# A decoder step with a 16384-expert mixer: the gate matrix grouped by 8 in DRAM, the sample's top-k on 128 partitions, PSUM copies of 8 tokens

## The chip, the cores and the metric

One core of a Trainium2 chip. The time is device microseconds of one execution; it is the median of three runs of the kernel. Engines are called TensorE (PE in the rows; PEld is its weight load), VectorE (DVE), ScalarE (ACT), GpSimd (POOL) and SyncE (SP, which here only issues DMAs).

## The reference

One layer for 512 prompt tokens and 64 sample tokens, width 1024: attention over three dilated windows beside a short gated convolution, an output projection, then a mixer of 16384 single-neuron experts, and a final norm. Only the mixer matters here. For each token and each of 8 heads:

```
q = (x @ wq) as 8 heads x 2 halves x 128
s = q . sub_keys                      128 scores per half
sv, si = top_k(s, 16)                 per half
cand = sv0[:, None] + sv1[None, :]    16 x 16 sums, top 16 of them
e = si0 * 128 + si1 of the winners;  g = softmax(top)
out = sum over 8 x 16 winners of  g * gelu(x . u[e]) * v[e]
```

## The kernel before, in words

The tokens are five blocks: 0 to 3 of 128 prompt tokens, and block 4, the 64 sample tokens. Blocks 0 and 4 take the mixer by gathering: for each winner a row of `u` and a row of `v` are fetched by an indirect DMA (`gather_units`, L464), and VectorE multiplies and adds them (tiles `jk` at L477 and `accg` at L487). Blocks 1 to 3 (`DENSE`, 384 tokens) take it densely: all 16384 experts are computed in 128 chunks of 128, and a matrix of gates, almost all zero, weighs them.

The stages around the change, in the order of the program:

1. `group(GB, ...)` (L576): output projection and norm of blocks 1 to 4; then the loop of L690 over 16 parts of `wq`: projection, scores (L703), a copy of the scores out of PSUM (L705, L707), and `topk1` (L490), five VectorE instructions per block and part. Block 4 has 64 tokens, so its instructions run on 64 partitions.
2. The gate build, `gbuild` (L812), for each dense block: `topk2` (L501) finds the 16 winners of each head. Then for each 8 tokens VectorE makes one-hot matrices `oj` and `oi` (L844, L848), ScalarE makes a third (L852, 8 instructions of 128 elements), TensorE multiplies them token by token into `pG` in PSUM (L857, L858, 128x128 each), and ScalarE copies `pG` to the tile `stg` (L860). A `stg` of 32 tokens goes to the DRAM tensor `Gd` (L863), 12 of them in all.
3. Between these stand the u-steps, `ustep` (L773): load a 128-expert chunk of `ut` (tile `ur`), split it on ScalarE (`uh`) and VectorE (`ul`), 24 multiplications into `pu` (L107 to L109), Gelu on ScalarE (tile `a`, L782), and for the first 62 chunks a store to `Ad`. 68 chunks run ahead of the last stage (`LAG`); `unext` calls them from the gate build by a count of debt.
4. `topk_gather` (L559) for block 4: `topk2` on 64 partitions, 8 heads; three DMAs then bring half of the slots to partitions 64 to 127 so that the gather uses all 128.
5. The v-loop (L935): for chunks 68 to 127 a u-step and a v-step, then for chunks 0 to 67 a v-step alone. A v-step (`vprep`, L885) loads `v`, loads the gates of four chunks at a time (`gt`, L891), multiplies them with the activations (tile `w`, L898), splits, and makes 18 multiplications of 512 columns into the accumulators `y` (L909 to L913).

`pump` (L448) places gather steps between all of these by a count of credit. The order of the instructions on each engine is not the order of the code: a scheduler with its own idea of times (L1031) sets it once, when the program is built. Each engine then works through its list in order. DMAs are issued from SyncE's list, those of the gather from GpSimd's.

The lines that matter most:

```
Gd = dram.tile([NTB, P, NCH, TB], F32, name="Gd")                      # L86: 12 x 128 x 128 x 32
pg_ = psG.tile([P, 4, P], F32, name="pG")                              # L854: 4 tokens, one PSUM bank
nc.scalar.activation(stg[:, :, tl:tl + 4].rearrange("p i t -> p t i"), pg_, AF.Copy, scale=1.0 / GSC)   # L860
nc.sync.dma_start(gt, Gd[:, :, i0:i0 + 4, :].rearrange("b j i t -> j b i t"))                           # L891
```

`stg` is [128, 128, 32]: the copy of L860 reads `pG` word after word and writes each word 128 bytes behind the last.

Of the kernel before, what the change touches and what calls it, by code (L numbers as in the profile page):

```python
# [19 lines left out]
P = 128  # L20
# [47 lines left out]
def body(tc, I, O):  # L68
# [12 lines left out]
    biasp = keep.tile([P, 4, P], F32, name="biasp")  # L81
# [4 lines left out]
    Gd = dram.tile([NTB, P, NCH, TB], F32, name="Gd")  # L86
# [28 lines left out]
    abp = pool(ab, "ab", side="right")  # L115
    qT = abp.tile([P, NPAIR, 512], F32, name="qT")
# [297 lines left out]
    zl = small.tile([P, 2, 18], F32, name="zl", bufs=1)  # L414
# [5 lines left out]
    zo = small.tile([P, 256], F32, name="zo", bufs=1)  # L420
# [69 lines left out]
    def topk1(st, cc, b, n, src):  # L490
        hd_, p_ = divmod(cc, 2)
# [9 lines left out]
    def topk2(st, b, n, ef, gat):  # L501
        sv, si = st[b]
        sf = tk.tile([P, 8, 2, 16], F32, name="sf")
        nc.vector.tensor_copy(sf[:n], si[:n])
        nc.vector.tensor_scalar(sf[:n, :, 0, :], sf[:n, :, 0, :], 128.0, None, op0=OP.mult)
        cand = tk.tile([P, 8, NCAND], F32, name="cand")
        cid = tk.tile([P, NCAND, 8], I16, name="cid")
        for src, dst in ((sv, cand), (sf, cid.rearrange("p w h -> p h w"))):
            o = 0
            for (a0, a1_, nb_) in PAIRS:  # L510
                na = a1_ - a0
                out = dst[:n, :, o:o + na * nb_].rearrange("p h (a b) -> p h a b", b=nb_)
                i0 = src[:n, :, 0, a0:a1_].unsqueeze(3).to_broadcast([n, 8, na, nb_])
                i1 = src[:n, :, 1, 0:nb_].unsqueeze(2).to_broadcast([n, 8, na, nb_])
                nc.vector.tensor_tensor(out, i0, i1, op=OP.add)
                o += na * nb_
            yield 1.2
        tv = tk.tile([P, 8, 16], F32, name="tv")
        tp = tk.tile([P, 8, 16], U32, name="tp")
        wc = tk.tile([P, NCAND], F32, name="wc", bufs=2)  # L520
        for hd_ in range(8):
            src = cand[:n, hd_, :]
            nc.vector.max(tv[:n, hd_, 0:8], src)
            nc.vector.match_replace(wc[:n], tv[:n, hd_, 0:8], src, -3.0e38)
            nc.vector.max(tv[:n, hd_, 8:16], wc[:n])
            nc.vector.max_index(tp[:n, hd_, 0:8], tv[:n, hd_, 0:8], src)
            nc.vector.max_index(tp[:n, hd_, 8:16], tv[:n, hd_, 8:16], wc[:n])
# [12 lines left out]
        yield 1.0  # L540
        efv = ef[:n].rearrange("p (h k) -> p h k", h=8)
        for k0 in (0, 8):
            w = FIRST[k0 + 7] + 1
            oh = tk.tile([P, NCAND, 8, 8], I16, name="oh")
            ohf = oh.rearrange("p w k h -> p w (k h)")
            sel = tf[:n, k0:k0 + 8, :].rearrange("p k h -> p (k h)").unsqueeze(1).to_broadcast([n, w, 64])
            nc.vector.tensor_tensor(ohf[:n, :w], iotaw[:n, :w], sel, op=OP.is_equal)
            yield 1.7
            nc.vector.tensor_tensor(oh[:n, :w], oh[:n, :w], cid[:n, :w].unsqueeze(2).to_broadcast([n, w, 8, 8]),
                                    op=OP.mult)  # L550
            yield 1.7
# [483 lines left out]
```

## Time and profile before

| | |
|---|---|
| time, median of 3 runs | 1880.66 us (1880.13 to 1886.15) |
| the profiled execution, span from first to last instruction | 1882.2 us |
| busy: TensorE, VectorE, ScalarE, GpSimd | 1738.2, 1430.9, 881.6, 579.0 us |
| mean granted TensorE clock | 0.955 of full |
| gate build, 816 to 1078 us | TensorE 231.2, VectorE 215.6, ScalarE 253.8 us busy of 262 |
| copies `stg` | 96, 101.2 us |
| DRAM traffic | 485.65 MB read, 45.63 MB written |

The page gives the span and no other time of the profiled execution; it is 1.5 us above the median of the runs. A stretch of the span is read with the view that gives each engine's busy time in it: where one engine is busy nearly all of the stretch, the others wait for it sooner or later; where TensorE is, its work alone sets the length. The view of waits then says who waited for whom. TensorE's busy time counts matmuls that overlap, so a group's mean duration (344 ns for `pu`) is longer than the distance from one to the next.

### The profile page before, as it was taken

What the parts mean: (1) busy time and instruction counts of PE and PEld (TensorE: products, weight loads), DVE (VectorE), ACT (ScalarE), POOL (GpSimd) and SP (SyncE); (2) the same over time, 40 slices, a digit from 0 to 9 for tenths busy, and PEclk for the clock granted to TensorE, in tenths of its full rate; (3) what the DMA queues carried; (4) which work ended last, traced back from release to release, by engine and by line L of the source; (5) the groups of instructions that cost most, each with busy time, mean ns of one, the idle gap of its engine ahead of it and who ended that gap; (6) DMA issues with size and microseconds to landing.
All of it is one profiled execution on the core that took longest, in us unless ns stands there. A gap on an engine that the chain in (4) does not pass through costs nothing. (4 is left out here: it accounts for less than half of the span.)

```text
span 1882.2 us, 29066 instructions
## 1 busy us (share of the span) xinstructions
PE 1738.2 (92%) x10391; PEld 1467.3 (78%) x10391; DVE 1430.9 (76%) x3064; ACT 881.6 (47%) x1615; POOL 579.0 (31%) x483
## 2 busy tenths in 40 slices
PE   7999899997679999988988999999999999999997
PEld 5778655654558998987978889999999997777776
DVE  5433235766888999998788578888888778888888
ACT  4222366645323333479999933333333333333334
POOL 1010201014554214311212234544444444333330
PEclk9999979978788999999999999999999999999999
DMA  4257569858898448867777699999999999999996
GB/s 143 100 181 288 208 245 337 316 185 291 302 320 302 154 143 312 277 216 267 266 261 250 253 365 330 353 335 348 331 336 341 320 361 334 363 344 367 340 349 210
DMA packets 199077, 533.75 MB, mean 284 GB/s; under 512 B 17586, under 2 KB 82660, under 8 KB 197268
## 3 DMA queue, kind: packets, MB, share of 16 engines
q1 hardware_dynamic: 133364, 294.22, 44.0%
q0 software_dynamic: 65568, 237.69, 35.5%
q8 instruction: 81, 1.33, 0.3%
q14 instruction: 64, 0.52, 0.1%
HBM read 485.65 MB, written 45.63 MB: 282 GB/s over the span
## 5 line engine op out<-in xcount | busy, mean ns | idle before, releaser
L469 POOL DMA_INDIRECT row<-in_u,idxg x192 | 257.9, 1343 | 457.6 <-DVE avg L477 231.4
L469 POOL DMA_INDIRECT row<-in_v,idxg x192 | 264.5, 1377 | 421.6 <-DVE accg L487 345.3
L107 PE MATMUL pu<-x2h,uh 128*128 128x384 f32 x1024 | 350.9, 343 | 21.4 <-ACT a L782 11.1
L109 PE MATMUL pu<-x2h,ul 128*128 128x384 f32 x1024 | 352.0, 344 | 7.5 <-DVE ul L104 7.3
L108 PE MATMUL pu<-x2l,uh 128*128 128x384 f32 x1024 | 348.8, 341 | 0.0
L103 ACT ACTIVATE vh<-vr 128x1024 fp32r<-128x1024 f32 x128 | 135.8, 1061 | 290.4 <-PE y L913 251.4
L477 DVE CUSTOM_DVE_ANT_0 jk<-row,x2g 128x1024 bf16<-128x1024 f32 x192 | 233.8, 1218 | 28.0 <-DMA row<-in_u,idxg 26.8
L487 DVE SCALAR_TENSOR_TENSOR accg<-row,avg,accg 128x1024 f32<-128x1024 f32 x190 | 243.2, 1280 | 7.7 <-DMA row<-in_v,idxg 6.7
L909 PE MATMUL y<-vh,wh 128*128 128x512 f32 x768 | 224.7, 395 | 15.5 <-ACT wh L103 15.5
L911 PE MATMUL y<-vl,wh 128*128 128x512 f32 x768 | 234.2, 393 | 0.0
L107 PEld LDWEIGHTS pu<-x2h,uh 128*128 128x128 f32 x1024 | 196.5, 192 | 27.1 <-ACT a L782 12.2
L104 DVE TENSOR_TENSOR vl<-vr,vh 128x1024 fp32r<-128x1024 f32 x128 | 156.6, 1224 | 77.9 <-ACT vh L103 74.9
L913 PE MATMUL y<-vh,wl 128*128 128x512 f32 x768 | 215.6, 390 | 0.0
L109 PEld LDWEIGHTS pu<-x2h,ul 128*128 128x128 f32 x1024 | 196.4, 192 | 12.4 <-DVE ul L104 10.1
L103 ACT ACTIVATE uh<-ur 128x1024 fp32r<-128x1024 f32 x128 | 136.0, 1064 | 145.1 <-PE pu L108 74.1
L108 PEld LDWEIGHTS pu<-x2l,uh 128*128 128x128 f32 x1024 | 196.3, 192 | 1.7
L104 DVE TENSOR_TENSOR ul<-ur,uh 128x1024 fp32r<-128x1024 f32 x128 | 156.2, 1220 | 35.9 <-ACT uh L103 34.2
L909 PEld LDWEIGHTS y<-vh,wh 128*128 128x128 f32 x768 | 143.9, 189 | 46.5 <-ACT wh L103 19.5
L911 PEld LDWEIGHTS y<-vl,wh 128*128 128x128 f32 x768 | 145.1, 189 | 30.4
L913 PEld LDWEIGHTS y<-vh,wl 128*128 128x128 f32 x768 | 144.0, 188 | 30.1
L104 DVE TENSOR_TENSOR wlo<-wraw,whi 128x1024 fp32r<-128x1024 f32 (+1 forms) x96 | 91.0, 952 | 67.5 <-ACT whi L103 67.1
L103 ACT ACTIVATE whi<-wraw 128x1024 fp32r<-128x1024 f32 (+1 forms) x96 | 79.8, 840 | 124.3 <-PE mm L109 53.7
(281 smaller groups left out, 2936.4 us busy)
## 6 DMA issues: line engine op xcount, KB each, us to landing
ur<-in_ut SPq DMA_DIRECT2D x128, 512.0 KB
vr<-in_v SPq DMA_DIRECT2D x128, 512.0 KB
kt<-in_ck SPq DMA_DIRECT2D x60, 512.0 KB
vt<-in_cv POOLq DMA_DIRECT2D x60, 512.0 KB
Gd<-stg SPq DMA_DIRECT2D x12, 2048.0 KB
gt<-Gd SPq DMA_DIRECT2D x32, 768.0 KB
wraw<-in_w_in SPq DMA_DIRECT2D x24, 512.0 KB
Ad<-a SPq DMA_DIRECT2D x62, 192.0 KB
```

Of the source, the lines that this page charges most:

```text
L103: nc.scalar.activation(hi, src, AF.Copy)
L104: nc.vector.tensor_tensor(lo, src, hi.bitcast(F32), op=OP.subtract)
L107: nc.tensor.matmul(out, ah, bh, start=first, stop=False)
L108: nc.tensor.matmul(out, ah, bl, start=False, stop=False)
L109: nc.tensor.matmul(out, al, bh, start=False, stop=last)
L469: nc.gpsimd.indirect_dma_start(out=r, out_offset=None, in_=I[src], in_offset=bass.IndirectOffsetOnAxis(ap=idx[:, s:s + 1], axis=0))
L477: nc.vector.tensor_tensor_reduce(jk, r, x2, 1.0, 0.0, OP.mult, OP.add, av[:, s:s + 1]))
L487: nc.vector.scalar_tensor_tensor(acc, r, av[:, s:s + 1], acc, op0=OP.mult, op1=OP.add))
L909: nc.tensor.matmul(accs[b][k], wh[:, sl], vh[:, k * 512:k * 512 + 512], start=first, stop=False)
L911: nc.tensor.matmul(accs[b][k], wh[:, sl], vl[:, k * 512:k * 512 + 512], start=False, stop=False)
L913: nc.tensor.matmul(accs[b][k], wl[:, sl], vh[:, k * 512:k * 512 + 512], start=False, stop=last)
```

## The change

Five edits:

- `Gd` gets the layout [16 groups of 8 chunks, 128, 12, 8, 32]. A store of `stg` becomes 16 pieces of 1 KB per partition where it was one of 16 KB; a load of gates (`gate_load`) brings a whole group of 8 chunks, 12 KB in a row per partition, where it was 12 pieces of 512 bytes for 4 chunks. There are 17 loads (the group of chunk 68 is read in two halves) where there were 32, and each is asked for four chunks ahead of its first use.
- Block 4's first top-k pass handles heads 0 to 3 on partitions 0 to 63 and heads 4 to 7 on partitions 64 to 127: the parts of `wq` come in the order 0, 8, 1, 9, ..., scores of the second of a pair are written to the upper partitions, and one `topk1` does both. `topk2` runs for it with 4 heads on 128 partitions, and two of the three DMAs that spread the slots go.
- `pG` holds 8 tokens (two PSUM banks), and one ScalarE copy does all 8: it writes 8 words in a row and reads words 512 bytes apart.
- The `ones` operand of the sums of squares in `group` has one column instead of 128.
- `biasp`, `zl` and `zo` come from other pools.

```diff
+GG = 8
-    ones = keep.tile([P, P], F32, name="ones")
+    ones = keep.tile([P, 1], F32, name="ones")
-    Gd = dram.tile([NTB, P, NCH, TB], F32, name="Gd")
+    Gd = dram.tile([NCH // GG, P, NTB, GG, TB], F32, name="Gd")
...
     def topk1(st, cc, b, n, src):
-        hd_, p_ = divmod(cc, 2)
+        hd_, p_ = divmod(cc % 8 if b == 4 else cc, 2)
...
-    def topk_gather(st, b, n, k):
...
+    def topk_gather(st, b, H, k):
+        ef = tk.tile([P, SLOTS], F32, name="ef", bufs=2)[:, :16 * H]
+        if H < 8:
+            nc.sync.dma_start(x2g[k][64:128, :], x2g[k][:64, :])
+        yield from topk2(st, b, H, ef, gatg[k][:, :16 * H])
+        nc.vector.tensor_copy(idxg[k][:, :16 * H], ef)
...
-                    nc.tensor.matmul(ss[:n, bi * P:bi * P + P], sq[:, c - c0, t0 - g0:t0 - g0 + n], ones,
+                    nc.tensor.matmul(ss[:n, bi:bi + 1], sq[:, c - c0, t0 - g0:t0 - g0 + n], ones,
...
-        for cc in range(16):
+        for cc in [c for lo in range(8) for c in (lo, lo + 8)]:
...
+                r0 = up_ if n < P else 0
+                nc.tensor.matmul(p2[r0:r0 + n, bi, :], qc[:, t0 - g0:t0 - g0 + n], skT[:, cc, :], start=True, stop=True)
+            nc.scalar.activation(sc, p2[:, :nb - 1, :], AF.Copy)
+            if not up_:
+                sc4 = gp.tile([P, P], F32, name="sc4", bufs=2)
+            nc.scalar.activation(sc4[up_:up_ + 64, :], p2[up_:up_ + 64, nb - 1, :], AF.Copy)
+            for bi, b in enumerate(grp[:-1]):
+                topk1(st, cc, b, P, sc[:, bi, :])
+            if up_:
+                topk1(st, cc, 4, P, sc4)
...
-                    nc.scalar.activation(stg[:, :, tl:tl + 4].rearrange("p i t -> p t i"), pg_, AF.Copy,
-                                         scale=1.0 / GSC)
+                nc.scalar.activation(stg[:, :, q * TQ:q * TQ + TQ], pg_.rearrange("p t i -> p i t"), AF.Copy,
+                                     scale=1.0 / GSC)
...
-            nc.sync.dma_start(Gd[di * (P // TB) + tb], stg)
+            nc.sync.dma_start(Gd[:, :, di * (P // TB) + tb].rearrange("g j i t -> j g (i t)"),
+                              stg.rearrange("p (g i) t -> p g (i t)", i=GG))
...
+    def gate_load(n_):
+        if n_ >= NCH or order[n_] in gtile or (n_ and order[n_ - 1] // GG == order[n_] // GG):
+            return
...
+        gt = vp.tile([P, NTB, GG, TB], F32, name="gt")
+        nc.sync.dma_start(gt[:, :, k0:k1], Gd[i0 // GG][:, :, k0:k1])
...
         vh, vl = load_split(I["v"][i * P:(i + 1) * P, :], vp, "v")
...
+        gate_load(n_)
+        gate_load(n_ + GG // 2)
+        gt = gtile.pop(i)
```

The scheduler is run anew, so the lists of all engines change. Three places of them follow.

ScalarE, the first tokens of the gate build before (`oi` are the third one-hot matrices of 8 tokens, `uh` and `a` belong to a u-step, `stg` is the copy):

```order
L852 ACTIVATE oi_7168<-oi_7166,gl 128x32x4 x8
L103 ACTIVATE uh<-ur 128x1024
L782 ACTIVATE a<-pu 128x384
L860 ACTIVATE stg<-pG 128x4x128 x2
L852 ACTIVATE oi_7241<-oi_7239,gl 128x32x4 x8
```

And now:

```order
L847 ACTIVATE oi_7126<-oi_7124,gl 128x32x4 x8
L103 ACTIVATE uh<-ur 128x1024
L777 ACTIVATE a<-pu 128x384
L852 ACTIVATE stg<-pG 128x128x8
L847 ACTIVATE oi_7197<-oi_7195,gl 128x32x4 x8
L852 ACTIVATE stg<-pG 128x128x8
L847 ACTIVATE oi_7230<-oi_7228,gl 128x32x4 x8
```

Two copies of 4 tokens became one of 8, and some groups of 8 tokens have no u-step between them.

ScalarE, the end of the gate build before (`vh` and `wh` open the v-loop):

```order
L860 ACTIVATE stg<-pG 128x4x128 x2
L103 ACTIVATE uh<-ur 128x1024
L782 ACTIVATE a<-pu 128x384
L103 ACTIVATE uh<-ur 128x1024
L782 ACTIVATE a<-pu 128x384
L103 ACTIVATE uh<-ur 128x1024
L103 ACTIVATE vh<-vr 128x1024
L103 ACTIVATE wh<-w 128x384
```

And now, the first rows of 33 that stand between the last copy and the first `wh`:

```order
L852 ACTIVATE stg<-pG 128x128x8
L103 ACTIVATE uh<-ur 128x1024
L777 ACTIVATE a<-pu 128x384 x3
L103 ACTIVATE uh<-ur 128x1024 x2
L103 ACTIVATE vh<-vr 128x1024
L777 ACTIVATE a<-pu 128x384 x2
L103 ACTIVATE vh<-vr 128x1024
L103 ACTIVATE uh<-ur 128x1024 x2
```

Behind the gate build there were 3 splits `uh` before the v-loop, and there are 15. Counted over TensorE's whole list, its 3072 multiplications into `pu` stand so (before, now): up to the last score multiplication of L703 83 and 25; from there to the first `pG` 663 and 529; from the first to the last `pG` 912 and 757; from there to the first `y` 94 and 385; in the v-loop 1320 and 1376. VectorE's list, likewise: gather steps ahead of the first `topk1` of blocks 1 to 4, 57 and 67; from there to the first `oj`, 44 and 28; from the first to the last `oj`, 34 and 27. Splits `ul` in the last two stretches: 27 and 20, then 39 and 31.

SyncE, in the v-loop, before:

```order
L891 DMA gt<-Gd 128x12x128
L767 DMA vr<-in_v 128x1024 x2
L896 DMA ar<-Ad 128x384 x2
```

And now:

```order
L887 DMA gt<-Gd 128x3072
L762 DMA vr<-in_v 128x1024 x2
L898 DMA ar<-Ad 128x384 x2
```

The load of gates keeps its place ahead of the loads of `v` and of the stored activations `ar`, in half as many places and with twice the bytes.

## Rows read from the trace of the kernel before

**Rows 1.** The page's first part: span, and each engine's busy time.

```profile
span 1882.2 us, 29066 instructions
PE 1738.2 (92%) x10391; PEld 1467.3 (78%) x10391; DVE 1430.9 (76%) x3064; ACT 881.6 (47%) x1615; POOL 579.0 (31%) x483
```

**Rows 2.** Busy time by stretch: length, PE, PEld, DVE, ACT, POOL (instructions), clock, DMA, GB/s.

```profile
440.00:586.00 146.00, 107.47 (x557) 78.47 (x558) 117.38 (x230) 52.63 (x100) 74.58 (x60) 0.80 0.90 322
586.00:816.00 230.00, 219.76 (x1195) 207.43 (x1196) 223.02 (x893) 83.22 (x139) 71.18 (x50) 0.99 0.67 223
816.00:1078.00 262.00, 231.15 (x1691) 218.84 (x1691) 215.58 (x441) 253.84 (x552) 55.80 (x32) 0.94 0.72 255
1078.00:1093.00 15.00, 15.00 (x89) 15.00 (x88) 4.85 (x4) 6.01 (x8) 0.00 (x0) 1.00 0.93 339
1093.00:1571.00 478.00, 474.83 (x2386) 429.60 (x2384) 395.12 (x450) 169.94 (x230) 223.95 (x169) 1.00 0.95 340
1571.00:1868.00 297.00, 284.72 (x1231) 232.74 (x1232) 248.90 (x317) 108.01 (x144) 100.47 (x77) 0.99 0.96 342
```

**Rows 3.** One stretch, `pu` alone (PE, PEld, ACT), then `pG` alone (PE, ACT).

```profile
816.00:1078.00 262.00, 183.83 (x917) 166.26 (x918) 19.36 (x39) 0.94 0.72 255
...
816.00:1078.00 262.00, 62.34 (x768) 100.21 (x96) 0.94 0.72 255
```

**Rows 4.** Waits of PE, 800 to 1110 us: total, times, longest.

```profile
PE pG L857 <- ACT stg L860: 11.8, 15, 5.1
PE pu L107 <- ACT a L782: 11.1, 5, 2.8
```

**Rows 5.** Timeline of ACT, 880 to 886 us: start, duration, instruction.

```profile
882.35 1.08 ACT L103 ACTIVATE uh<-ur 128x1024 fp32r<-128x1024 f32 x1
...
883.66 2.10 ACT L860 ACTIVATE stg<-pG 128x512 f32<-128x512 f32 x2
885.52 2.46 ACT L852 ACTIVATE oi<-oi,gl 128x128 f16<-128x128 f16 x8
```

**Rows 6.** Timeline of PE, first and last of ten multiplications into `pG`.

```profile
919.83 0.22 PE L857 MATMUL pG<-oi,oj 128*128 128x128 f16 x1
...
920.39 0.23 PE L858 MATMUL pG<-oi,oj 128*128 128x128 f16 x1
```

**Rows 7.** ACT groups by shape: count, busy us, mean ns, idle before them.

```profile
L103 ACT ACTIVATE vh<-vr 128x1024 fp32r<-128x1024 f32 x128 | 135.8, 1061 | 290.4 <-PE y L913 251.4 <-issue 28.2 <-DMA vr<-in_v 7.3
...
L860 ACT ACTIVATE stg<-pG 128x512 f32<-128x512 f32 x96 | 101.2, 1163 | 5.0 <-PE pG L858 5.0
...
L264 ACT ACTIVATE PTs<-sT 128x512 f32<-128x512 f32 x24 | 14.2, 591 | 11.2 <-PE sT L259 11.1
...
L332 ACT ACTIVATE kT<-pT 128x256 f32<-128x256 f32 x5 | 1.9, 390 | 5.0 <-PE pT L320 5.0
...
L328 ACT ACTIVATE qbd<-pT 64x256 f32<-64x256 f32 x2 | 0.8, 378 | 1.7 <-PE pT L320 1.7
```

**Rows 8.** DVE groups by shape: count, busy us, mean ns.

```profile
L477 DVE CUSTOM_DVE_ANT_0 jk<-row,x2g 128x1024 bf16<-128x1024 f32 x192 | 233.8, 1218 | 28.0 <-DMA row<-in_u,idxg 26.8 <-DVE sv L497 0.3 <-DVE rdp L203 0.2
...
L104 DVE TENSOR_TENSOR ul<-ur,uh 128x1024 fp32r<-128x1024 f32 x128 | 156.2, 1220 | 35.9 <-ACT uh L103 34.2 <-PE pu L109 1.4
...
L515 DVE TENSOR_TENSOR cid<-sf 128x64 int16<-128x64 f32 x8 | 5.3, 663 | 0.0
...
L495 DVE MAX8 sv<-scs 64x8 f32<-64x128 f32 x16 | 4.4, 275 | 0.0
...
L515 DVE TENSOR_TENSOR cand<-sv 128x64 f32<-128x64 f32 x8 | 1.7, 212 | 0.0
...
L531 DVE CAST tf<-tp 128x128 int16<-128x128 uint32 x4 | 1.2, 292 | 0.0
...
L533 DVE TENSOR_TENSOR te<-tv 128x128 f32<-128x128 f32 x4 | 1.1, 270 | 0.0
```

**Rows 9.** Waits of SyncE's queue, 1110 to 1882 us: total, times, longest.

```profile
SPq L891 <- DVE w L898: 18.3, 8, 3.9
```

More of the change, by code (lines that the diff above doesn't have):

```diff
@@ L499, in topk1, with topk2 @@
         nc.vector.max_index(ix[:, 8:16], v[:, 8:16], w[:n])
-    def topk2(st, b, n, ef, gat):
+    def topk2(st, b, H, ef, gat):
         sv, si = st[b]
[L503 to L507, printed above, removed]
+        K = 8 * H
+        sf = tk.tile([P, 8, 2, 16], F32, name="sf")[:, :H]
+        nc.vector.tensor_copy(sf, si)
+        nc.vector.tensor_scalar(sf[:, :, 0, :], sf[:, :, 0, :], 128.0, None, op0=OP.mult)
+        cand = tk.tile([P, 8, NCAND], F32, name="cand")[:, :H]
+        cid = tk.tile([P, NCAND * 8], I16, name="cid")[:, :NCAND * H].rearrange("p (w h) -> p w h", h=H)
         for src, dst in ((sv, cand), (sf, cid.rearrange("p w h -> p h w"))):
@@ L517, in topk2 @@
             yield 1.2
-        tv = tk.tile([P, 8, 16], F32, name="tv")
-        tp = tk.tile([P, 8, 16], U32, name="tp")
+        tv = tk.tile([P, 8, 16], F32, name="tv")[:, :H]
+        tp = tk.tile([P, 8, 16], U32, name="tp")[:, :H]
         wc = tk.tile([P, NCAND], F32, name="wc", bufs=2)
[L521 to L527, printed above, removed]
+        for hd_ in range(H):
+            src = cand[:, hd_, :]
+            nc.vector.max(tv[:, hd_, 0:8], src)
+            nc.vector.match_replace(wc, tv[:, hd_, 0:8], src, -3.0e38)
+            nc.vector.max(tv[:, hd_, 8:16], wc)
+            nc.vector.max_index(tp[:, hd_, 0:8], tv[:, hd_, 0:8], src)
+            nc.vector.max_index(tp[:, hd_, 8:16], tv[:, hd_, 8:16], wc)
@@ L699, in group @@
             p2 = psc()
-            sc = gp.tile([P, 4, P], F32, name="scs", bufs=2)
+            sc = gp.tile([P, 3, P], F32, name="scs", bufs=2)
+            up_ = cc // 8 * 64
             for bi, b in enumerate(grp):
                 t0, n = BLKS[b]
-                nc.tensor.matmul(p2[:n, bi, :], qc[:, t0 - g0:t0 - g0 + n], skT[:, cc, :], start=True, stop=True)
-            full = [bi for bi, b in enumerate(grp) if BLKS[b][1] == P]
-            nc.scalar.activation(sc[:, :len(full), :], p2[:, :len(full), :], AF.Copy)
-            if len(full) < nb:
-                nc.scalar.activation(sc[:64, nb - 1, :], p2[:64, nb - 1, :], AF.Copy)
-            for bi, b in enumerate(grp):
-                n = BLKS[b][1]
-                topk1(st, cc, b, n, sc[:n, bi, :])
+                r0 = up_ if n < P else 0
[8 more added lines that the diff above has]
+                topk1(st, cc, 4, P, sc4)
             pump(PUMP_GB)
@@ L714, in mkst @@
     def mkst(pl, grp):
-        return {b: (pl.tile([P, 8, 2, 16], F32, name=f"sv{b}"), pl.tile([P, 8, 2, 16], U32, name=f"si{b}"))
-                for b in grp}
+        return {b: tuple(pl.tile([P, 4 if b == 4 else 8, 2, 16], dt, name=f"{nm}{b}")
+                         for nm, dt in (("sv", F32), ("si", U32))) for b in grp}
     st0 = mkst(keep2, GA)
@@ L814, in gbuild @@
         gt = tk.tile([P, SLOTS], F32, name="gt", bufs=2)
-        yield from topk2(st, b, P, ef, gt)
+        yield from topk2(st, b, 8, ef, gt)
         ei = tk.tile([P, SLOTS], I32, name="ei")
@@ L873, in body @@
         unext()
-    drain(topk_gather(st, 4, 64, 1))
+    drain(topk_gather(st, 4, 4, 1))
     bg.append(gather_units(1, SLOTS // 2))
@@ L883, in body, with vprep @@
     gtile = {}
-    def vprep(i, a):
-        vh, vl = load_split(I["v"][i * P:(i + 1) * P, :], vp, "v")
-        key = (i // 4, i >= LAG)
-        if key not in gtile:
-            gt = vp.tile([P, NTB, 4, TB], F32, name="gt")
-            i0 = i // 4 * 4
-            nc.sync.dma_start(gt, Gd[:, :, i0:i0 + 4, :].rearrange("b j i t -> j b i t"))
-            gtile[key] = gt
-        gt = gtile[key]
+    def gate_load(n_):
+        if n_ >= NCH or order[n_] in gtile or (n_ and order[n_ - 1] // GG == order[n_] // GG):
+            return
+        i0 = order[n_]
+        k0 = i0 % GG
+        k1 = GG
+        while order[min(n_ + k1 - k0, NCH) - 1] != i0 + k1 - k0 - 1:
+            k1 -= 1
+        gt = vp.tile([P, NTB, GG, TB], F32, name="gt")
+        nc.sync.dma_start(gt[:, :, k0:k1], Gd[i0 // GG][:, :, k0:k1])
+        for k in range(k0, k1):
+            gtile[i0 - k0 + k] = gt[:, :, k, :]
+    def vprep(n_, i, a):
+        vh, vl = load_split(I["v"][i * P:(i + 1) * P, :], vp, "v")
+        gate_load(n_)
+        gate_load(n_ + GG // 2)
+        gt = gtile.pop(i)
         if a is None:
@@ L939, in body @@
             a = akeep.get(i)
-        v = vprep(i, a)
+        v = vprep(n_, i, a)
         if n_ < NCH - 2:
```

80 lines of the change are left out of this document (31 added, 49 removed).

## The prediction

> **What bounds the kernel now.** I first read the page's busy times: TensorE is busy for 1738.2 of 1882.2 us, VectorE for 76%, ScalarE for 47% [rows 1]. A time that TensorE fills to 92% falls only where TensorE stands still or runs at its lower clock, so the second view is the busy time by stretch, cut at the places where the lists change their kind of work [rows 2]. From 1093 to 1571 us (u-steps and v-steps) TensorE is busy for 474.8 of 478 at full clock: that stretch is worth nothing to anybody who does not take work from TensorE. From 586 to 816 (scores and top-k) TensorE has 219.8 of 230 and VectorE 223.0: both are close to full. The gate build, 816 to 1078, is different: ScalarE has 253.8 of 262, 97%, while TensorE has 231.2 at a granted clock of 0.94.
>
> How much of those 231.2 does TensorE need? The stretch 1078 to 1093 holds nothing but multiplications into `pu`, 89 in 15.00 us, so one takes 0.169 us at full clock [rows 2]. Nine steps of `pG` lie between 919.83 and 920.39, 0.062 us each [rows 6]. The gate build holds 912 of the first in TensorE's list and 768 of the second (the trace shows 917 and 768 in its window [rows 3]): 912 x 0.169 + 768 x 0.062 = 154 + 48 = 202 us. So 60 of the 262 us are standing still and slow clock. The view of waits says for whom TensorE waits there: first for the copy `stg`, 11.8 us, then for `a`, 11.1 us, both ScalarE's [rows 4]. ScalarE bounds the gate build. Per 8 tokens it spends 2.46 us on `oi` and 2.10 us on two copies, besides the u-steps' splits [rows 5].
>
> **The copy.** In the window 96 copies take 100.2 us of ScalarE [rows 3], 1.163 us each [rows 7]. A copy of the same 512 words out of PSUM that writes them in a row takes 0.591 (`PTs`). So the copy pays 0.57 us for its steps, and they are all in the write. The new copy writes 8 words in a row, then steps 128 bytes. That form is in the trace: `qbd` is written in runs of 8 words 128 bytes apart, 256 words in 0.378 us, against 0.390 for `kT` with 256 words in a row [rows 7]. The write becomes free. The step moves to the read, which takes words 512 bytes apart from PSUM, and no row of ScalarE shows that. Bounds: from below the price of 1024 words without steps, 1.061 us (`vh`); from above the price per word of today's copy. From 0.591 and 1.061 a word costs 0.918 ns and an instruction 0.121 us; today's copy costs (1.163 - 0.121) / 512 = 2.035 ns a word, so 1024 words 2.20 us. The nearest rows on reads are VectorE's: `tf`, which reads 128 words 64 bytes apart, takes 292 ns where `te` without steps takes 270; `cid`, which steps in what it writes, takes 663 where `cand` with as many elements takes 212 [rows 8]. Steps cost in writes and hardly in reads, so I take 1.06 us.
>
> [...]
>
> **The sum, stretch by stretch.** The lists were made anew, and u-steps moved: what counts is the work that each engine now has in each stretch.
>
> - *Before 586.* Ten gather steps of 1.22 us [rows 8] now stand ahead of the top-k that stood behind it: 12 us more for VectorE, which was busy for 117.4 of 146 [rows 2]. Between 0 and +12; I take **+8**. `ones` with one column falls here too, where TensorE has 38 us of idle time: nothing, and nothing if that cover goes but a shorter multiplication behind the same weight load. The moved pools cost no instruction.
> - *586 to 816.* TensorE loses 83 + 663 - 25 - 529 = 192 multiplications: 219.8 - 32.4 = 187 us. VectorE loses 16 gather steps and 7 splits at 1.22 us, and 8 rounds of 5 top-k instructions of the sample at 0.275 (64 partitions cost the same as 128, so one for two is a plain gain) [rows 8]: 223.0 - 19.5 - 8.5 - 11 = 184 us. Both were at 95 to 97% of the stretch; at 94% it takes 199: **-31** (between -20, at 89%, and -42, both full).
> - *Gate build.* ScalarE: 253.8 - 100.2 + 48 x 1.06 = 204.5, and seven u-steps fewer at 1.06 + 0.50 us (`uh` as `vh`; `a` 19.36 us for 39) [rows 3, 7]: 193.6. VectorE: 215.6, less 8 splits and 7 gather steps: 197.3. TensorE needs 757 x 0.169 + 48 = 176. At its 97% ScalarE would finish in 200, but then VectorE would be as full as it: what is late next is VectorE. I take 206: **-56** (from -62 to the rivals' values).
> - *Behind the gate build.* 385 multiplications stand there, not 94: TensorE works alone, 291 x 0.169 = **+49**. Under it lies what else moved: the sample's second top-k pass, now with half the heads, its gather's start without two DMAs, and the last store of gates, 2 MB in pieces of 1 KB. I cost these at nothing; if this run of TensorE were not there, the v-loop's first gates would wait for that store, some 6 us at 339 GB/s [rows 2].
> - *v-loop to 1571.* 56 multiplications more on a full TensorE: **+9.5**.
> - *From 1571.* TensorE has 12 us of idle time to give; DMA is at 0.96. The loads of gates carry the same bytes in pieces of 12 KB and no longer hold up SyncE's queue for a buffer, 18.3 us of waiting in front of other loads [rows 9]. Against that, each now puts 0.75 MB more at a time ahead of `ar` and `vr`: 2.2 us at 342 GB/s, nine times, at worst 20. Between -12 and +20; nearest is the wait that goes: **-4**.
>
> Sum: 8 - 31 - 56 + 49 + 9.5 - 4 = -24.5. Against the profiled span of 1882.2 that is 1857.7; the median of the runs is 1.5 lower than that span, so I forecast **1856 us**. The 60 us of u-steps that leave the first two stretches come back whole: what is gained is TensorE's idle time in the gate build, 60 before and 206 - 176 = 30 after. With every term at its own ends but the copy at 1.06, the forecast's own range is 1836 to 1876. A measurement of this kernel can tell about 0.3%, 5.6 us, from no change.
>
> **Rivals.**
>
> *A. The read pays for its steps.* At 2.20 us a copy, 48 take 105.8 us, ScalarE has 253.8 - 100.2 + 105.8 - 10.9 = 248.5, and the gate build takes 256, 6 less than now. But the scheduler has already put 60 us of TensorE's work behind it. Sum: 8 - 31 - 6 + 49 + 9.5 - 4 = +25.5, **1906 us: slower**. It decides at the price where the gate build takes 230: 230 x 0.97 - (253.8 - 100.2 - 10.9) = 80 us for 48, 1.67 us a copy; above it the change loses. For it: today's copy pays for one side's steps, and the read side of PSUM is not shown. Against it: `tf`. Chance 0.25.
>
> *B. VectorE takes ScalarE's place.* With 197 us of work it needs 206 only if it is 96% busy, as it was from 586 to 816; in the gate build it has been 82% busy, and at that it would take 240. Midway, 223, the sum is -7.5: **1873 us**, and up to 1890 at 240. For it: its one-hot matrices have two buffers each, which ScalarE and TensorE must first have read. Against it: those waits were for a ScalarE that was full. Chance 0.15.
>
> *Forecast*, chance 0.60. That the change does not do what it says is excluded by the lists: 48 copies of 1024 words stand where 96 stood.
>
> **Numbers.** Of the forecast's 0.60, 0.56 lie below 1875 and 0.04 within 0.3%; of B's 0.15, 0.06, 0.06 and 0.03 slower; of A's 0.25, 0.02 and 0.23. Faster 0.62, same 0.12, slower 0.26. The range reaches from the forecast's lower end, 1836, to A's value, 1906; about 0.05 lies below and 0.10 above.
>
> **What would show it.** The copy's row: near 1.06 us for 128x1024, ScalarE's gate build near 194 us, its length near 206. Then a full TensorE for some 65 us until the first `y`. Wrong if the copy takes over 1.67; if it takes 1.06 and the gate build still over 225 with VectorE named in TensorE's waits (B); or if 1571 to the end is longer than 297, which would be the larger loads.

## The result, and the profile after

The change takes 1897.4 us (median of 4 runs, 1892.5 to 1900.7) against 1880.4 us: a ratio of 1.0077, interval 1.0056 to 1.0098. It is slower by 0.8%, and the forecast of 1856 us, faster, was wrong. The range, up to 1906, holds it by luck: its upper end is the time with a slow copy, and the copy costs what was forecast. The page's first part and the copy's group:

```profile
span 1895.7 us, 28790 instructions
...
PE 1754.9 (93%) x10391; PEld 1469.3 (78%) x10391; DVE 1416.6 (75%) x2966; ACT 841.9 (44%) x1565; POOL 563.8 (30%) x483
```

```profile
L852 ACT ACTIVATE stg<-pG 128x1024 f32<-128x1024 f32 x48 | 49.4, 1032 | 9.5 <-PE pG L851 8.9 <-issue 0.6
```

ScalarE does 40 us less than in [rows 1]. TensorE is busy 17 us longer with as many instructions, and idle 3 us less: the same work took it longer. To see where, the run is cut at five starts that both traces have. Before, by tile (shortest, median and longest duration in ns, first and last start in us):

```profile
L593 ACT ACTIVATE x2h<-cat,ga x8: 653/656/658, 478.8 to 482.7; 128x448 fp32r<-128x448 f32 x8
L857 PE MATMUL pG<-oi,oj x384: 217/223/312, 815.8 to 1077.0; 128*128 128x128 f16 x192
L860 ACT ACTIVATE stg<-pG x96: 1040/1168/1304, 819.1 to 1077.8; 128x512 f32<-128x512 f32 x96
L909 PE MATMUL y<-vh,wh x768: 387/389/628, 1094.9 to 1867.5; 128*128 128x512 f32 x192
L898 DVE TENSOR_TENSOR w<-ar,gt x62: 547/552/622, 1571.2 to 1836.7; 128x384 f32<-128x384 f32 x62
```

and with the change:

```profile
L585 ACT ACTIVATE x2h<-cat,ga x8: 657/659/661, 500.6 to 504.5; 128x448 fp32r<-128x448 f32 x8
L850 PE MATMUL pG<-oi,oj x384: 218/224/328, 800.6 to 1020.8; 128*128 128x128 f16 x192
L852 ACT ACTIVATE stg<-pG x48: 1004/1027/1086, 803.7 to 1021.2; 128x1024 f32<-128x1024 f32 x48
L911 PE MATMUL y<-vh,wh x768: 387/389/632, 1103.3 to 1880.9; 128*128 128x512 f32 x192
L900 DVE TENSOR_TENSOR w<-ar,gt x62: 546/553/579, 1589.6 to 1850.1; 128x384 f32<-128x384 f32 x62
```

The stretches are a (to the first `x2h`), b (to the first `pG`), c (the gate build, to the start of the last `stg`), d (to the first `y`), e (to the first `w` from `ar`) and f (to the end). Lengths alone mislead, because u-steps were moved from one to another. So I take 0.169 us [rows 2] for each `pu` multiplication off the stretch that holds it; what is left can be compared, and sums to the span less the same 3072 x 0.169 = 519 us in every kernel. **This table carries the rest of the document**: ratios to the kernel before with their intervals, counts of `pu` in b, c, d and e from the lists, a and f as they are, b to e without their `pu` time, from one profile each. The counts part c from d at the last `pG`; up to 13 multiplications run between that and the last `stg`, so that c can be up to 2.2 us shorter than the table has it, and d longer by as much.

| run | ratio [interval] | pu in b / c / d / e | a | b | c | d | e | f |
|---|---|---|---|---|---|---|---|---|
| before | | 746 / 912 / 94 / 1320 | 478.8 | 210.9 | 107.9 | 1.2 | 253.2 | 311.0 |
| the change | 1.0077 [1.0056, 1.0098] | 554 / 757 / 385 / 1376 | 500.6 | 206.4 | 92.7 | 17.0 | 253.8 | 306.1 |
| e1 copy | 0.9994 [0.9971, 1.0018] | 746 / 766 / 170 / 1390 | 477.8 | 214.3 | 90.7 | 11.5 | 253.3 | 310.7 |
| e2 places | 1.0142 [1.0111, 1.0173] | 602 / 947 / 131 / 1392 | 495.4 | 212.3 | 109.0 | 2.1 | 253.2 | 311.7 |
| e3 top-k | 1.0080 [1.0052, 1.0108] | 663 / 862 / 131 / 1416 | 476.5 | 214.7 | 111.3 | 2.4 | 254.5 | 315.0 |
| e4 copy, top-k | 1.0011 [0.9993, 1.0028] | 663 / 720 / 313 / 1376 | 480.9 | 211.0 | 88.7 | 16.3 | 252.6 | 309.9 |
| f1 all, old places | 0.9947 [0.9923, 0.9970] | 674 / 757 / 265 / 1376 | 476.9 | 211.6 | 87.0 | 13.8 | 253.9 | 304.3 |
| f2 e4, WSTEP 2 | 0.9904 [0.9876, 0.9932] | 674 / 910 / 112 / 1376 | 476.0 | 214.7 | 84.6 | 3.6 | 252.6 | 316.6 |
| f3 all but groups | 1.0132 [1.0102, 1.0161] | 554 / 757 / 385 / 1376 | 494.3 | 206.4 | 89.3 | 15.4 | 253.2 | 318.8 |
| f4 PUMP_S 0 | 1.0319 [1.0282, 1.0356] | 554 / 742 / 400 / 1376 | 490.4 | 185.9 | 87.7 | 18.2 | 248.4 | 394.0 |
| g1 zo back | 1.0011 [0.9994, 1.0028] | 674 / 718 / 304 / 1376 | 491.2 | 206.1 | 89.4 | 17.5 | 255.2 | 305.6 |
| g2 g1, WSTEP 2 | 0.9954 [0.9933, 0.9974] | 674 / 862 / 120 / 1416 | 492.3 | 209.1 | 87.6 | 6.3 | 257.2 | 305.6 |
| g3 f1, WSTEP 2 | 0.9842 [0.9820, 0.9865] | 674 / 912 / 138 / 1348 | 485.5 | 212.6 | 84.7 | 1.2 | 254.3 | 304.5 |
| g4 copy, WSTEP 2 | 0.9886 [0.9864, 0.9908] | 746 / 862 / 115 / 1349 | 478.0 | 212.3 | 79.5 | 4.4 | 252.5 | 305.7 |
| h1 before, WSTEP 2 | 1.0006 [0.9982, 1.0030] | 746 / 936 / 70 / 1320 | 479.1 | 211.2 | 102.3 | 4.1 | 253.7 | 308.7 |
| h2 ones | 1.0036 [1.0012, 1.0060] | 722 / 923 / 107 / 1320 | 483.1 | 208.5 | 112.4 | 2.2 | 252.1 | 310.4 |

From the first row to the second: a +21.8, b -4.5, c -15.2, d +15.8, e +0.6, f -4.9, together +13.6, the difference of the spans. The loss lies **ahead of the first `x2h`** and **behind the gate build**. One profile is good to a few us: nine of these kernels (before, e1, e3, e4, f1, f2, g3, g4, h1) have the same lists of TensorE and VectorE up to the last 20 or so of the instructions ahead of the first `x2h`, which comes between 476.0 and 485.5.

**Stretch a.** Four stretches of 20 us each, before and then with the change (columns as in [rows 2]):

```profile
440.00:460.00 20.00, 16.79 (x157) 9.63 (x157) 12.68 (x34) 10.44 (x29) 11.59 (x12) 0.91 0.90 316
460.00:480.00 20.00, 10.46 (x44) 5.72 (x43) 11.10 (x24) 7.33 (x17) 7.93 (x8) 0.58 1.02 381
480.00:500.00 20.00, 14.15 (x82) 12.13 (x82) 19.54 (x39) 12.73 (x22) 11.20 (x9) 0.82 0.74 247
500.00:520.00 20.00, 14.71 (x54) 11.32 (x55) 17.22 (x35) 1.35 (x3) 10.25 (x10) 0.83 0.88 318
```

```profile
440.00:460.00 20.00, 14.93 (x144) 8.25 (x143) 10.33 (x27) 7.77 (x22) 9.89 (x9) 0.78 0.99 347
460.00:480.00 20.00, 13.60 (x44) 6.85 (x45) 13.22 (x33) 9.84 (x24) 10.39 (x9) 0.50 0.74 249
480.00:500.00 20.00, 16.70 (x62) 9.54 (x59) 15.48 (x34) 8.01 (x18) 11.68 (x11) 0.50 0.77 247
500.00:520.00 20.00, 10.97 (x49) 9.57 (x48) 14.73 (x22) 10.40 (x16) 6.28 (x6) 0.50 0.77 277
```

TensorE is busy as long in both, 56.1 and 56.2 us of 80, but with the change at a granted clock of 0.50 for three slices, and it gets 299 multiplications (of several kinds) done instead of 337. The clock falls at 451 us:

```profile
450.00:451.00 1.00, 0.75 (x18) 0.55 (x19) 0.00 (x0) 0.56 (x1) 0.69 (x2) 1.00 0.99 389
451.00:452.00 1.00, 1.00 (x6) 0.77 (x5) 0.00 (x0) 0.43 (x1) 0.89 (x1) 0.54 1.04 410
```

What stood around the drop, in the timelines of VectorE and TensorE:

```profile
459.09 1.23 DVE L478 CUSTOM_DVE_ANT_0 jk<-row,x2g 128x1024 bf16<-128x1024 f32 x1 [4.86 <-DMA row<-in_u,idxg]
460.24 0.69 DVE L199 CUSTOM_DVE_ANT_0 sc<-mm,biasp 128x512 f32<-128x512 f32 x1
```

```profile
450.25 0.64 PE L272 MATMUL sT<-vt,PTs 128*32 128x128 f32 x16 [2.39 <-DMA vt<-in_cv]
460.99 2.07 PE L215 MATMUL mm<-kT,qT 64*128 64x512 f32 x2 [2.44 <-DVE mxp L199]
```

Just ahead of the drop TensorE has waited 2.39 us for a late `vt`. Behind it VectorE stands 4.86 us for a gathered row with an attention's maximum next in its list, and TensorE waits for that maximum. Before, POOL's list has six row gathers, the last two `vt` loads, then the other rows; now four rows, `vt`, three rows, `vt`, one row, `vt`: the last `vt` come behind more rows on one queue. VectorE's list now has 31 gather steps ahead of the first `x2l` instead of 18, and 12 maxima of the prompt's attention behind the first of them instead of 7.

This stretch of 80 us is not the whole of it. The 40th of the 48 maxima of the prompt's attention, before and then with the change:

```profile
435.00 0.56 DVE L198 CUSTOM_DVE_ANT_0 sc<-mm,biasp 128x384 f32<-128x384 f32 x1
```

```profile
447.90 0.56 DVE L199 CUSTOM_DVE_ANT_0 sc<-mm,biasp 128x384 f32<-128x384 f32 x1
```

So 13 of the 22 us are there before this drop of the clock, and 9 come behind. And from the start to the first `x2h`, in the kernel before, the change, f3 (whose early list is that of the change; the experiments follow) and f4 (without gather steps in the attention); then, in e1, whose early list is that of before, from 440 us to its first `x2h`:

```profile
0.00:478.80 478.80, 429.91 (x3438) 298.64 (x3438) 240.51 (x763) 220.71 (x479) 71.78 (x115) 0.92 0.64 232
```

```profile
0.00:500.60 500.60, 444.06 (x3448) 304.20 (x3448) 256.46 (x790) 223.24 (x483) 88.62 (x129) 0.89 0.65 233
```

```profile
0.00:494.30 494.30, 433.98 (x3448) 298.56 (x3448) 256.15 (x790) 222.74 (x483) 90.36 (x129) 0.92 0.66 237
```

```profile
0.00:490.40 490.40, 447.20 (x3448) 307.40 (x3448) 223.90 (x734) 222.43 (x483) 56.15 (x101) 0.90 0.59 213
```

```profile
440.00:477.80 37.80, 31.57 (x184) 17.03 (x182) 21.69 (x52) 15.54 (x40) 17.84 (x15) 0.56 0.87 302
```

The change has all three: TensorE idle for 56.5 us instead of 48.9, a clock of 0.89 instead of 0.92, and VectorE 16 us busier, which is the 13 gather steps more. But f3 is 15.5 us late at the clock of before, f4 is 11.6 late with less work for VectorE and less idle time for TensorE than before, and e1 runs its last 38 us at 0.56, where before had 0.76, and is not late. The list makes the lateness; how it divides among these three is not settled.

**Stretch d.** Waits from 1021 to 1103 us, then SyncE's queue in the same place:

```profile
PE pu L107 <- ACT uh L103: 9.8, 2, 6.9
ACT uh L103 <- DMA ur<-in_ut: 8.4, 5, 4.0
```

```profile
1030.10 0.46 SPq L762 DMA_DIRECT2D vr<-in_v  x1
1031.61 2.15 SPq L887 DMA_DIRECT2D gt<-Gd  x2
1033.81 0.55 SPq L762 DMA_DIRECT2D vr<-in_v  x1
1034.46 0.71 SPq L781 DMA_DIRECT2D Ad<-a  x1
1035.22 0.88 SPq L762 DMA_DIRECT2D vr<-in_v  x1
1036.15 0.90 SPq L898 DMA_DIRECT2D ar<-Ad  x2
1037.15 2.21 SPq L762 DMA_DIRECT2D ur<-in_ut  x2
```

```profile
1050.64 1.06 ACT L103 ACTIVATE uh<-ur 128x1024 fp32r<-128x1024 f32 x1 [4.03 <-DMA ur<-in_ut]
```

When the gate build ends, the v-loop's memory comes free and its first loads, `vr` three times, two of gates and `ar` twice, are issued within 7 us, ahead of two `ur`; `uh` is made from the first of these 13 us later. TensorE, for which 385 multiplications stand there, is busy 6.52, 4.81 and 8.00 us in the slices of 10 from 1030 to 1060. Over the stretch it is idle for 11.3 us; the rest of what d loses goes with a clock of 0.94:

```profile
1021.00:1103.00 82.00, 70.68 (x387) 68.79 (x385) 35.55 (x36) 27.69 (x37) 14.76 (x12) 0.94 0.82 286
```

**Stretch c.** TensorE in the gate build, 801 to 1021: all, `pu` alone, `pG` alone.

```profile
801.00:1021.00 220.00, 204.90 (x1530) 187.44 (x1528) 193.89 (x402) 202.56 (x490) 34.78 (x29) 0.96 0.82 279
```

```profile
801.00:1021.00 220.00, 157.83 (x758) 135.13 (x758) 15.80 (x32) 0.96 0.82 279
...
801.00:1021.00 220.00, 70.99 (x766) 48.40 (x47) 0.96 0.82 279
```

All three engines are now 88 to 93% busy, and nothing much is waited for: TensorE's longest entry is 6.5 us for `ul`, and 0.5 for `stg` instead of 11.8 [rows 4].

### The profile page after: what moved, and what is told of

The parts are those of the page before. It is cut to its first block, busy times and chain, and to the rows that moved or that the text cites. A ratio compares the mean times of both kernels' runs of the same rounds, so it can differ in the third digit from the quotient of the medians.

```text
span 1895.7 us, 28790 instructions
## 1 busy us (share of the span) xinstructions
PE 1754.9 (93%) x10391; PEld 1469.3 (78%) x10391; DVE 1416.6 (75%) x2966; ACT 841.9 (44%) x1565; POOL 563.8 (30%) x483
## 5 line engine op out<-in xcount | busy, mean ns | idle before, releaser
L470 POOL DMA_INDIRECT row<-in_u,idxg x192 | 244.2, 1272 | 519.6 <-DVE avg L478 281.1
L107 PE MATMUL pu<-x2h,uh 128*128 128x384 f32 x1024 | 351.0, 343 | 16.3 <-ACT uh L103 10.7
L915 PE MATMUL y<-vh,wl 128*128 128x512 f32 x768 | 224.6, 390 | 0.0
L103 ACT ACTIVATE wh<-w 128x384 fp32r<-128x384 f32 x128 | 67.0, 525 | 208.2 <-DVE w L900 169.9
```

The lines of the kernel that those rows point to most:

```text
L103: nc.scalar.activation(hi, src, AF.Copy)
L107: nc.tensor.matmul(out, ah, bh, start=first, stop=False)
L470: nc.gpsimd.indirect_dma_start(out=r, out_offset=None, in_=I[src], in_offset=bass.IndirectOffsetOnAxis(ap=idx[:, s:s + 1], axis=0))
L915: nc.tensor.matmul(accs[b][k], wl[:, sl], vh[:, k * 512:k * 512 + 512], start=False, stop=last)
```

## The experiments

None leaves out work. An edit said to be "as in the diff" is the hunk of the change's diff.

**e1, the copy alone**, as in the diff (`pg_` of 8 tokens, one copy).

> The kernel before with one part of the change: one copy of 8 tokens, 8 words in a row, in place of two copies of 4. Up to the gate build the lists are those of before, instruction for instruction; the gate build holds 766 pu multiplications instead of 912, and 76 more stand behind it and 70 more in the v-loop. Theory 1 (the loss of the whole change comes from the re-made order ahead of the gate build, and from what stands behind it): the first x2h stays at 479 +-2 us, the copy takes 1.03 us, the gate build shrinks from 262 to 220 +-8 us, the 146 multiplications come back as 25 us, and the time is 1864 +-8 us. Theory 2 (a shorter gate build is given back behind it, because the stage behind it has to wait for loads, whatever the order): the stretch behind the gate build is over 30 us longer and the time is 1878 to 1890 us.

0.9994: no change, theory 2's time, but by neither theory alone. The first `x2h` comes at 477.8, the gate build takes 220.2 us (262 before), so the copy gains 17 us net there; d costs 10 net more, and b 3. The 146 multiplications that left the gate build came back as 25 us. The profile's sum, 5 us less than before, is less than e1's runs differ by, 1868.9 to 1890.2.

**e2, the places alone.**

```
-    biasp = keep.tile(...)
+    biasp = abp.tile(...)
-    zl = small.tile(...)
+    zl = a1.tile(...)
-    zo = small.tile(...)
+    zo = a1.tile(...)
```

> The kernel before with one part of the change: only where three small tiles lie (biasp in the pool of the attention's tiles, zl and zo in the pool of the first projections). No instruction is added, removed or resized, but the lists differ from VectorE's 185th row on. Theory 1 (order): where these tiles lie decides the order of the lists, and with it the loss: the first x2h comes 10 to 25 us later than 479, and the time is 1890 to 1905 us. Theory 2 (what is lost is the price of operations that the change adds or resizes): nothing of that kind is here, x2h at 479 +-3, and the time is 1880 +-5 us.

1.0142. Not an instruction differs, and the kernel is 27 us slower. `x2h` comes at 495.4, with the signature of the change:

```profile
460.00:480.00 20.00, 12.46 (x43) 6.36 (x43) 11.14 (x30) 7.34 (x20) 6.55 (x7) 0.50 0.79 248
480.00:500.00 20.00, 12.40 (x51) 7.22 (x51) 12.21 (x24) 10.22 (x21) 11.89 (x10) 0.59 0.87 296
```

That is theory 1. With `biasp` alone moved the lists stay word for word those of before; in the whole change, `zl` put back alone alters no row either. It is `zo`, 1 KB a partition, that makes the early list anew.

**e3, the sample's top-k alone**, and **e4, with the copy**, as in the diff.

> The kernel before with one part of the change: the sample's top-k packed on 128 partitions. Up to the scores the lists are those of before. 133 pu multiplications leave the stretches ahead of the gate build's end (83 the scores, 50 the gate build), 37 stand more behind it, 96 in the v-loop: 22 us of TensorE. Theory 1 (order): x2h at 479 +-2, VectorE loses 40 top-k instructions of 0.275 us and half of the sample's second pass, some 16 us in all, of which about 10 lie on the path: 1870 +-8 us. Theory 2 (the packing puts a price on the score stage: two passes' scores in one tile, which VectorE's list waits for): the scores' stretch does not shrink by more than TensorE's work that left it (14 us), and the time is 1880 to 1892 us.

> The kernel before with two parts of the change, the copy of 8 tokens and the sample's packed top-k; gates in groups of 4, ones 128x128 and the tiles where they were before. Up to the scores the lists are those of before. Theory 1 (order): x2h at 479 +-2; the gate build near 215 us; 313 multiplications stand behind it, which TensorE does in 53 us if it is full; the sum of the two parts' gains, 1855 +-10 us. Theory 2 (what stands behind the gate build waits for loads whatever the order): behind the gate build over 65 us and a time of 1875 to 1890 us.

1.0080 and 1.0011, slower than theory 1 said in both, and e3, at 1895.9 us, slower than theory 2 too. With the old early lists `x2h` stays at 476.5 and 480.9. The packing gains nothing: in e3 stretch b falls by 10 us where 14 us of TensorE's work left it, as theory 2 said. That e3 is 0.8% slower is spread over b, c and f, 3 to 4 us each; no cause was found. In e4 the stretch d takes 69 us with 313 multiplications, 16 more than at full rate: theory 2's number.

**f1, the whole change with the old places**: `biasp`, `zl`, `zo` as before, `ones` 128x128, `KEEP = 4`. **f3, all but the groups of 8** (gates laid out and loaded as before).

> The whole change, but biasp, zl and zo lie where they lay before and ones is 128x128; four instead of six of the kept a tiles make room for the larger gates (two more stores and loads of 196 KB). Up to the scores the lists are those of before; 757 pu multiplications in the gate build, 265 behind it, 1376 after. Theory 1 (the 22 us lost ahead of the first x2h come from where the small tiles lie, which decides the order): x2h at 479 +-3; the rest as in the whole change; 1875 +-6 us. Theory 2 (they come from the edits themselves, whatever the order): x2h at 492 or later, and 1892 to 1902 us.

> The whole change, but the gates lie in DRAM as before and are loaded in groups of 4. The lists are those of the whole change up to the v-loop. Theory 1 (the larger loads of gates at the v-loop's start hold up u-step loads behind the gate build): that stretch, 82 us for 385 multiplications, loses 17 us of standing still and falls by 5 to 8; the end from the first w from ar, 306 us, is 4 to 6 longer again, since SyncE's queue waits for gate buffers; in sum no change, 1895 +-5 us. Theory 2 (the larger groups are a plain gain or loss of over 8 us): a time below 1888 or above 1905 us.

f1 takes 0.9947 of the time of before, 1.3% under the change, and a is back at 476.9: theory 1. It puts back `ones` and changes `KEEP` too, so e2 and g1 tell more of the places alone. f3's 1908.5 us are theory 2's: the groups of 8 are a gain, 0.5% by the two ratios, and f tells where, 318.8 without and 306.1 with them (304.3 to 305.6 in the other runs with groups but f4, 305.7 to 316.6 in those without). The larger loads are not what d waits for (15.4 and 17.0).

**f4, no gather steps in the attention**: `PUMP_S = 0`.

> The whole change with PUMP_S 0: no gather step is handed out among the attention's units, only the four row gathers that find free buffers can stand among the vt loads. Theory 1 (the gather steps cause the loss ahead of x2h: row gathers stand among the last vt loads in POOL's queue, jk steps ahead of the prompt attention's maxima in VectorE's list, TensorE stands still and drops to the lower clock): x2h at 480 or earlier, clock 0.8 or more from 440 to 500 us; what it costs later is VectorE's time in the score stretch, and the time is 1875 to 1895 us. Theory 2 (the attention's own order is slow, with or without gather steps): x2h at 495 or later and 1895 to 1915 us.

1.0319, slower than both theories said: the steps that are not taken there lengthen the end by 88 us. For stretch a it falls between the theories: `x2h` at 490.4, 10 us of the 22 back. The clock is low all the same, while POOL has nothing to do and VectorE little:

```profile
460.00:480.00 20.00, 16.19 (x61) 8.90 (x61) 3.68 (x16) 11.55 (x30) 0.00 (x0) 0.58 0.01 4
480.00:500.00 20.00, 14.62 (x73) 10.29 (x71) 10.08 (x17) 12.89 (x23) 0.00 (x0) 0.67 0.28 100
```

So the gather steps are at most about half of it; against f3, which shares the change's early list and has `x2h` at 494.3, they are 4 us of 15.5. The rest I put down to the prompt's attention that the new list leaves for the end, where nothing else fills TensorE's gaps; that is argued, not shown.

**g1, the change with `zo` in `small`**, and **h2, `ones` with one column alone**.

> The whole change with one word taken back: zo, 1 KB per partition, lies in the pool small again instead of a1. Nothing else. The lists are then those of the kernel before in the attention but for a few places (19 gather steps ahead of the first x2l instead of 31; before has 18), 718 pu multiplications in the gate build, 304 behind it. Theory 1 (where zo lies made the order, and with it the 22 us): x2h at 479 +-3 and 1873 +-6 us. Theory 2 (another part of the change does it): x2h at 492 or later and 1890 us or more.

> The kernel before with one part of the change: ones has one column, and 48 multiplications of 128x128 become 128x1. All else is as before, but the lists differ from TensorE's 1326th row on: 21 gather steps stand ahead of the first x2l instead of 18, and 8 prompt maxima behind the first gather step instead of 7. Theory 1 (any edit that makes the early list anew has a price of its own, and the 12 us that remained with zo taken back are that of ones): x2h at 488 to 493 and 1888 +-6 us. Theory 2 (a shorter multiplication behind the same weight load costs nothing): x2h at 479 +-4 and 1880 +-5 us.

g1 is level with before, 1.0011: one word gives back 11 us of median. But `x2h` comes at 491.2, not 479, between the theories: its early list is a third one. h2 is 1.0036, theory 1's time, with `x2h` at 483.1, between the theories and within what the nine kernels with the old list show. So `ones`, for which I had put nothing, is not free either: it too makes the lists anew. Which stretch pays for it, and its share in g1, isn't settled.

**WSTEP 2**, which puts u-steps back into the gate build: **f2** (e4 with it), **g2** (g1), **g3** (f1), **g4** (e1) and **h1** (the kernel before with it alone).

```
-WSTEP = 4
+WSTEP = 2
```

> The kernel with the copy and the packed top-k (e4), with WSTEP 2 instead of 4, which puts u-steps back into the gate build: 910 pu multiplications there instead of 720, 112 behind it instead of 313. Theory 1 (u-steps that stand behind the gate build wait there for their loads among the v-loop's first ones, 16 us in e4): the gate build takes 32 us more (190 x 0.169), the stretch behind it 48 less, and the time falls by 10 to 16, to 1870 +-6 us. Theory 2 (with ScalarE, VectorE and TensorE all over 88% busy the gate build pays more than 0.169 us for a multiplication put back): it takes over 42 us more, and the time is 1880 to 1890 us.

> The kernel g1 with WSTEP 2: 862 pu multiplications in the gate build, 120 behind it, 1416 after. Theory 1 (u-steps behind the gate build cost what they wait there, those within it 0.169 us a multiplication): the gate build near 234 us, the stretch behind it near 25, and a time 8 to 14 us under g1, 1862 +-6 us. Theory 2 (the shorter stretch behind it only moves the v-loop's first loads into the gate build, and what was saved comes back at the end): within 4 us of g1.

> The kernel f1 (whole change, small tiles in their old places, four kept a tiles) with WSTEP 2: 912 pu multiplications in the gate build, 138 behind it, 1348 after. Theory 1: the gate build near 242 us, the stretch behind it near 27, and a time 8 to 14 us under f1, 1862 +-6 us. Theory 2, as for g2: within 4 us of f1.

> The kernel with the copy of 8 tokens alone (e1), with WSTEP 2: 862 pu multiplications in the gate build instead of 766, 115 behind it instead of 170, 1349 after instead of 1390. Theory 1 (the copy alone gained nothing because the scheduler put u-steps behind the gate build, where they wait): the waiting behind the gate build falls from 11 us to 4 or less, and the time to 1870 +-6 us. Theory 2 (the copy's gain is given back whatever stands where): 1880 +-5 us.

> The kernel before with WSTEP 2 and nothing else: 936 pu multiplications in the gate build instead of 912, 70 behind it instead of 94, the rest as before. Theory 1 (in the kernel before ScalarE bounds the gate build and nothing waits behind it, so that more u-steps there gain nothing; only with the shorter copy does it pay to put them back): the gate build 262 to 270 us, 1880 +-6 us. Theory 2 (WSTEP 2 is a gain of its own, by which the runs with it are faster): 1870 us or less.

WSTEP 2 alone does nothing (1.0006); the copy alone does nothing (0.9994); the two together gain 1.1% (0.9886). In all four kernels with the new copy it gains (1.1% from e4 to f2, from f1 to g3 and from e1 to g4, 0.6% from g1 to g2), and what d loses falls from between 11.5 and 17.5 us to between 1.2 and 6.3. In direction that is theory 1 in all five, with a larger gain than it said in f2, g3 and g4. Not all its numbers came: g2, at 1875.7 us, missed 1862 because g1 was slower than assumed, and h1's gate build took 260.5 us, not 262 to 270. A multiplication put back costs less than 0.169: from e4 to f2 the gate build grows by 28.0 us for 190, 0.147 each, and TensorE's idle time there falls by 4 us.

**The best, g3**, is f1 with WSTEP 2: 1854.1 us median, 0.9842. Its gate build, stretch behind it and v-loop, in the slowest of its five runs:

```profile
812.00:1050.80 238.80, 227.79 (x1689) 212.83 (x1689) 208.28 (x416) 210.76 (x501) 40.25 (x34) 0.97 0.83 288
1050.80:1075.30 24.50, 23.99 (x139) 23.67 (x138) 11.60 (x14) 9.18 (x14) 2.96 (x3) 1.00 0.99 354
1075.30:1557.40 482.10, 478.99 (x2411) 433.98 (x2409) 393.25 (x447) 171.16 (x230) 224.00 (x168) 1.00 0.92 337
```

As many `pu` multiplications stand in this gate build as in that of before, in 239 us instead of 262, and TensorE is busy 24.0 of 24.5 us behind it.

## Why the prediction was wrong

Three steps failed: the moved pools at no cost, the gate build at 206 us, and a full TensorE behind it. Together with a stretch b that was 6 us shorter than forecast they make up the 38 us between the forecast -24.5 and the +13.5 of the profiles.

- **The copy: right.** 1.06 us forecast, 1.032 measured, 0.5 us of TensorE's waiting left of 11.8. The read takes 1.01 ns for each of its words 512 bytes apart in PSUM, the instruction's fixed part included, no more than `vh`, which reads SBUF without steps, 1.04 [rows 7]. The first rival is refuted, though its total of 1906 came nearer than mine.
- **"Before 586", +8: wrong by 14.** The step that failed is "The moved pools cost no instruction", which was true and no argument: they cost 27 us by themselves (e2), 17 of them ahead of the first `x2h`. I counted VectorE's ten gather steps and gave TensorE 38 us of cover. The made-over list puts 13 more of them and more of the prompt's attention close ahead of the first `x2h`; TensorE waits longer, and it runs at a granted clock of 0.50 from 460 to 520 us. But f3 is 15.5 us late at the average clock of before, and f4 11.6 us late without gather steps there, so the share of each stays open. `ones` at nothing was wrong too (h2).
- **586 to the gate build, -31: right within 6.** b became 37.0 us shorter, 32.4 of that by moved multiplications; net, it changed by -4.5 instead of +1.4. In the kernel before, `MAX8` of L495 takes 277 ns on 128 partitions and 275 on 64 [rows 8]; the packing by itself still gained nothing (e3).
- **Gate build, 206: measured 220.6.** Two terms were too small. "TensorE needs 176" took the best rate of each kind of step. [Rows 3] already had those of the whole gate build, though groups overlap in them, 183.83 us for 917 `pu` and 62.34 for 768 `pG`, 0.200 and 0.081 each; with the change it is 157.83 / 758 = 0.208 and 70.99 / 766 = 0.093, and TensorE is busy 204.9 of 220. And ScalarE has 202.6 instead of 193.6. In the trace of before, `oi` alone and `uh` alone in the same window:

```profile
816.00:1078.00 262.00, 62.34 (x768) 61.75 (x92) 112.67 (x371) 0.94 0.72 255
...
816.00:1078.00 262.00, 165.82 (x611) 115.66 (x612) 47.49 (x39) 41.88 (x39) 0.94 0.72 255
```

  With `stg` and `a` [rows 3] that is 112.67 + 41.88 + 100.21 + 19.36 = 274.1 us of ScalarE in a window where it is busy for 253.8: neighbours overlap at their ends, and taking a group's whole busy time off the engine's takes off too much. The engine that came next was all three together, not VectorE alone: the second rival, at 223 us, came near in length with another cause.
- **Behind the gate build, a full TensorE for 65 us: measured 82.** The step that failed is "TensorE works alone, 291 x 0.169 = +49": it became +65. Under "I cost these at nothing" I looked for a wait of the v-loop on the gates' store; it was the u-steps that waited, for their own loads behind the v-loop's first. That the order of the loads does it is read from the queue; no run moved the loads alone. Every kernel with the new copy and 170 or more multiplications behind the gate build loses 11 to 18 us there, and WSTEP 2, which leaves 112 to 138, brings that down to 1 to 6.
- **v-loop +9.5 and from 1571, -4: right**, 10.0 and -4.9. The direction was taken from a wait, [rows 9], and f3's profile puts 12.7 us on the groups there, though f differs by as much among the kernels without groups.

The three misses, 14, 15 and 16 us, have a pattern: I priced TensorE at its full rate, or gave it cover, wherever the lists put its work, and in each place it waited for others or ran slower. With the places put back and WSTEP 2 the kernel takes 0.9842 of before, about 1851 us: the forecast's size, by removing two of its three misses. The forecast's own range was also added up too narrow: with every term at its own end, and the gate build from 200 to 206, it is 1823 to 1895 us, not 1836 to 1876.

## What to carry to other kernels

Compare kernels whose scheduler makes the lists anew by stretch and net of the work that was moved; and where an edit touches a pool, look at the lists before crediting the edit: the place of a tile of 1 KB a partition was worth more than the copy. When an engine that bounded a stretch becomes faster, set the amount of work interleaved there again: copy and WSTEP gained nothing alone and 1.1% together. Work "moved behind" a stage was not free here, where the next stage's first loads are issued at that moment: 11 to 18 us of loss in the kernels with the new copy and 170 or more multiplications there.

## What was not expected of the hardware

- ScalarE's read from PSUM in steps of 512 bytes costs nothing that shows: 1.032 us for 1024 words with the change, 1.061 for the 1024 that `vh` reads without steps [rows 7]. The step costs in SBUF's write: in the kernel before, 1.163 us for 512 words 128 bytes apart, 0.591 in a row [rows 7].
- TensorE stayed at 0.50 from 460 to 520 us while it was busy 13.60, 16.70 and 10.97 us of each 20, and was given 0.58 and 0.67 in f4 while it was busy 16.19 and 14.62 from 460 to 500.
